# A two-layer diffusion backbone on one core: where the gate blocks, the query sums, the second norm's root and the token weights stand

## The chip, the cores and the metric

The kernel runs on one core of one Trainium2 chip. TensorE (PE) multiplies, with its weight loads (PEld) shown apart; VectorE (DVE), ScalarE (ACT) and GpSimd (POOL) do the rest; SyncE (SP) issues the DMA loads from one in-order queue. The metric is the device time of one execution in microseconds (us), and the median over several executions is compared.

## The reference

Two layers run over 512 latent tokens and 256 context tokens of width 1024. Each layer is a half-step feed-forward, a mixing part, and a second half-step feed-forward; ahead of each stands an RMS norm with a shift and a scale, behind each a gate, all nine of them made from a conditioning vector.

```python
def half_ffn(h, g, shift, scale, gate, wg, wu, wd):
    return h + 0.5 * gate * swiglu(modulate(rms_norm(h, g), shift, scale), wg, wu, wd)

for l in range(DEPTH):
    need_ctx = l < DEPTH - 1
    ml = jnp.split(s_lat @ w_mod[l] + b_mod[l], N_MOD, axis=-1)     # mc: the same from s_ctx
    x = half_ffn(x, ..., ml[0], ml[1], ml[2], ...)                  # ctx with mc
    y_l, y_c = token_mixing(modulate(rms_norm(x, ..), ml[3], ml[4]), ...)
    x = x + ml[5] * y_l
    x = half_ffn(x, ..., ml[6], ml[7], ml[8], ...)                  # ctx too if need_ctx
```

`token_mixing` projects the tokens, runs six heads of grouped-query attention, a short gated convolution and six heads of latent attention (its queries come from a normed, compressed 384-wide query), and projects the concatenation back. In the last layer the context is not carried on past the keys and values.

## The kernel before, in words

Activations lie transposed: eight tiles `xT[k]` of 128 features by 768 tokens (latent and context). Every fp32 weight and activation is split into a high and a low part (`wh`/`wl`, or two slots `s`); a product is three matmuls, high by high, high by low, low by high (`mm3`). A weight block is loaded to `wr` (two buffers), cast by ACT to the high part, and subtracted by DVE to give the low part (`wsplit`). PSUM has two large buffers (`ps`) and four small ones (`po`). Buffers of a tag are used in turn. An instruction issued while an engine is "chained" keeps the written order on that engine; elsewhere a scheduler orders the instructions by readiness and written order.

The 128 modulation blocks (`mod_queue`) are taken in a fixed order, each with one load to `mr` (two buffers) and one or two sums on DVE (`junk`, one for each of the two conditioning vectors). `pump(n)` takes the next `n` blocks, `pump(upto=...)` all up to a named one. `(l, 8)` is the gate of the second feed-forward of layer `l`. `mixing` pumps up to `(l, 5)`, `(l, 7)` and `(l, 6)` at its end, and then calls `residual` for the output projection with `npump=1`: one block behind each of the five output tiles that come before the held ones. `ffn` pumps up to its gate after its first chunk of activations, ahead of the first update of `xT`.

`residual` multiplies activations by a down or output projection, adds the gated result to `xT`, and makes the normed input `h` of the next part. It has two streams of columns, `c0` (latent) and `c1` (context; in the last mixing part, the two halves of the latent tokens). The last `ntail` output tiles are held: 6 in a feed-forward that is followed by another part, 3 in the output projection. Their `c0` columns are done first; their `c1` columns are cut into units, one for each held tile and input block, which `run(n)` strews as filler on PE. The tail then goes:

- `run(4)`, and the column sums of the squares of `c0` on PE (`count_steps`, matmuls with a vector of ones); the mean and the root on DVE (`rsqrt`, eight small instructions); `run(7)`; the spread of the root by four transposes; `run(5)`.
- a loop over `k` from 0 to 8: `scaled(k)` (DVE), `high(k)` (ACT), `low(k-1)` (DVE) make `h`; `products(k-1)` on PE are the first products of the next part with blocks `E`; updates and squares of `c1` and `run(3)` come behind them. From `k == 2` on the squares of `c1` are counted, and at `k == 7` the mean and root of `c1` are made and spread. `hold` is 4 with six held tiles, 6 with three: products past it come after the spread. With three held tiles the third block of `E` is cast and subtracted at `k == 6`.
- a loop over `k` for `h` in `c1`, in which the first feed-forward's tail also prepares the token weights (`wn_late`, one 384-wide block for each `k`, `LATE`).

`mixing` makes the token projections from those blocks, the compressed keys and queries (`comp`, loop over `i`), and their sums of squares (`stats`). Just ahead of attention stand `evac`, the splits of keys and queries, `uq(0)` (the first tile of up-projected queries, with the counts of the query's squares between its products) and the mean. `attend` then runs the units, each with two query blocks: `scores`, `maxima` (DVE), `exps` (ACT), `transposes`, `high`, `low`, `values`. Further work is put at places of a unit by `at(n, place, ...)` ("mid", "b", "end"); `uq(1)` stands at unit 0's "mid".

Of the kernel before, what the change touches and what calls it, by code (L numbers as in the profile page):

```python
# [8 lines left out]
F32 = mybir.dt.float32  # L9
F32R = mybir.dt.float32r  # L10
I32 = mybir.dt.int32
AF = mybir.ActivationFunctionType
# [3 lines left out]
P = 128  # L16
D = 1024
KD = D // P
SEQ = 512
CTX = 256  # L20
T = SEQ + CTX
NLT = SEQ // P
NT = T // P
# [15 lines left out]
NWR = 2  # L39
DUE = (1, 1, 1, 1, 2)  # L40
PRE = {1: (0, 1), 5: (2,), 7: (3,)}
LAG = 1
LATE = {k: 1 for k in range(8)}
NATIVE = (0, 2)


# [1 line left out]
def tile_net(ctx: ExitStack, tc: tile.TileContext, a, out):  # L48
    nc = tc.nc
# [33 lines left out]
    te, ve, se, pe = Engine(nc.tensor, "te"), Engine(nc.vector, "ve"), Engine(nc.scalar, "se"), nc.gpsimd  # L83

    const = ctx.enter_context(tc.tile_pool(name="const", bufs=1))
    pool = ctx.enter_context(tc.tile_pool(name="pool", bufs=1))
# [4 lines left out]
    def nm(s):  # L91
        uid[0] += 1
        return f"{s}{uid[0]}"

    def slot(dt=F32, w=T):
        return pool.tile([P, w], dt, name=nm("s"), tag="s", bufs=NSLOT)
# [4 lines left out]
    def small(w, dt=F32, tag="sm", bufs=12):  # L101
        return pool.tile([P, w], dt, name=nm("m"), tag=tag, bufs=bufs)
# [7 lines left out]
    def f32(t):  # L110
        return t.bitcast(F32)
# [11 lines left out]
    zeros = const.tile([P, 2 * NT], F32, name="zeros")  # L123
# [69 lines left out]
    def wload(src, w):  # L193
        raw = pool.tile([P, 1024], F32, name=nm("wr"), tag="wr", bufs=NWR)
        nc.sync.dma_start(out=raw[:, :w], in_=src)
        return raw

    def wsplit(raw, w, hi=None, lo=None, eng=None):
        if hi is None:
            hi = pool.tile([P, 1024], F32R, name=nm("wh"), tag="wh", bufs=3)  # L200
            lo = pool.tile([P, 1024], F32R, name=nm("wl"), tag="wl", bufs=3)
        se.copy(hi[:, :w], raw[:, :w])
        (eng or ve).tensor_sub(lo[:, :w], raw[:, :w], f32(hi)[:, :w])
        return hi, lo
# [21 lines left out]
    def wblock(src, w=1024):  # L226
        return wsplit(wload(src, w), w)
# [89 lines left out]
    def rsqrt(ms, n, tag="rs", bufs=3):  # L317
        y, steps = rsqrt_steps(ms, n, tag, bufs)
        for f in steps:
            f()  # L320
        return y

    class Stats:
# [41 lines left out]
        def sums(self, *more):  # L365
            self.zero()
            for n, sq in enumerate((self.acc,) + more):
                self.count(sq, n == len(more))
# [53 lines left out]
    def residual(blocks, rhs, gate, streams, nxt, pre=None, late={}, view=nv, npump=0, ntail=3):  # L422
# [7 lines left out]
        ntail = ntail if two else 0  # L430
# [13 lines left out]
        S = [Stats(cols, D, (po, ps)[n]) for n, (cols, i) in enumerate(streams)]  # L444
# [11 lines left out]
        raws = [wload(src, 1024) for src in pre[:2]]  # L456
        E = []
# [22 lines left out]
        s1, ready, tiles = [], [], {}  # L480
        units = [(n, k) for n in range(ntail) for k in range(nk)]

        def run(count):
            for _ in range(count):
                if not units:
                    return
                n, k = units.pop(0)
                if k == 0:
                    if n % 2 == 0:
                        tiles[n // 2] = ps()  # L490
                project(packed(tiles[n // 2][:, BANK * (n % 2):BANK * (n % 2 + 1)], c1, view), held[n][1], rhs, [k])
                if k == nk - 1:
                    ready.append(n)
# [20 lines left out]
                s1.append(sq)  # L514

        squared = [0, None]
        run(4)
        for n, f in enumerate(S[0].count_steps(S[0].acc, S[0].sq)):
            f()
            if n % 3 == 2:  # L520
# [18 lines left out]
        hold = 4 if ntail == 6 else 6  # L539
        prev = None  # L540

        def products(k):
            for n in range(len(accs)):
                lat_mm(accs[n], E[n], h, k, c0, hview)

        for k in range(KD + 1):
            if k < KD:
                cur = HMod(h[k], k, c0, R, A[i0][:, k:k + 1], B[i0][:, k:k + 1], hview)
                cur.scaled()
                cur.high()  # L550
            if k == 6 and len(E) == 2:
                E.append(wsplit(raws[2], 1024))
            if prev is not None:
                prev.low()
                if k <= hold or k == KD:
                    products(k - 1)
            prev = cur
            second_update()
            second_square()
            run(3)  # L560
            if k == 2:
                S[1].zero()
                S[1].count(S[1].acc, False)
            if k >= 2:
                for _ in range(2 if k < 7 else len(s1)):
                    if s1:
                        S[1].count(s1.pop(0), not (s1 or ready or updated or units))
            if k == 7:

                S[1].mean()  # L570
                r1 = rsqrt(S[1].ms, S[1].w // P)
                R1 = po()
                for j in range(S[1].w // P):
                    te.transpose(out=R1[:, j * P:(j + 1) * P], in_=r1[:, j:j + 1].to_broadcast([P, P]), identity=ident)
                if len(accs) == 2:
                    accs.append(po())
                    for kk in range(hold):
                        lat_mm(accs[2], E[2], h, kk, c0, hview)
                for kk in range(hold, 7):
                    products(kk)  # L580
        prev = None
        for k in range(KD + 1):
            if k < KD:
                cur = HMod(h[k], k, c1, R1, A[i1][:, k:k + 1], B[i1][:, k:k + 1], hview)
# [6 lines left out]
            prev = cur  # L591
# [598 lines left out]

    def wn_late(l, wn):

        k, both = len(wn), slot(F32R)
        hi, lo = both[:, 0:384], both[:, 384:768]
        wn.append((hi, lo))
        raw = wload(a["wiN"][l, k, :, 0:384], 384)
        se.copy(hi, raw[:, 0:384])
        return lambda: ve.tensor_sub(lo, raw[:, 0:384], f32(hi))

    def mixing(l, hin, early, streams, nxt, pre):  # L1200
        h, E, accs = hin
# [53 lines left out]
        for c0, w, nt in ((0, 384, nqt), (384, 288, NT)):  # L1255
            if c0:
                conv(1)
            wn = []
            for k in range(KD):
                wn.append(early.pop(0) if c0 == 0 and early else wn_block(l, k, c0, w))  # L1260
            for t in range(nt):
# [21 lines left out]
                lo = 0 if t < nqt else 384  # L1283
# [87 lines left out]
        for i in range(5):  # L1371
            name, g, w = ("ckv", gckv[:, i:i + 1], T) if i < 2 else ("cq", gcq[:, i - 2:i - 1], wq)
            pt = ps()
            project(natural(pt, slice(0, w)), wb, h,
                    between=stats["ckv"].count_steps(stats["ckv"].acc, stats["ckv"].sq) if i == 3 else ())
            if i < 4:
                wb = wblock(a["wiT"][l, i + 1])
            else:
                wuq.append(wsplit(wload(a["wuq"][l, 0], 864), 864,
                                  *(pool.tile([P, 1024], F32R, name=nm("we"), tag="mr", bufs=2) for _ in range(2))))  # L1380
                wuq.append(wblock(a["wuq"][l, 1], 864))
            for f, t in ramp[i]:
                f(t)
            if i == 3:
                stats["ckv"].mean()
            elif i == 4:
                rr["ckv"] = rsqrt(stats["ckv"].ms, NT)
            if i < 4:
                evac(pt, name, g, w)
                stats[name].square(pt[:, :w])  # L1390
                if i != 1:
                    stats[name].accumulate()
# [42 lines left out]
        key_split(k1, slot(F32R), pool.tile([P, T], F32R, name=nm("k2"), tag="mscr", bufs=1))  # L1435
        query_split(q0, 1)
        stats["cq"].accumulate()


        st3 = pool.tile([P, NT, 18], F32, name=nm("st3"), tag="st3", bufs=1)  # L1440
# [19 lines left out]
        def uq(t, between=()):  # L1460
            q = slot()
            q_tok.append(q)
            sq = temp()
            pt = ps().rearrange("p (f c) -> p f c", f=2)
            up([pt[:, f, :288] for f in range(2)], t, comp["cq"], 288, wuq, between)
            se.copy(q[:, :576].rearrange("p (f c) -> p f c", f=2), pt[:, :, :288])
            se.activation(out=sq[:, :576].rearrange("p (f c) -> p f c", f=2), in_=pt[:, :, :288], func=AF.Square)
            sv = sq[:, :576].rearrange("p (h d) -> p h d", d=96)

            def sums():  # L1470
                ve.tensor_reduce(out=st3[:, t, 0:6], in_=sv[:, :, 0:64], axis=AX.X, op=ALU.add)
                ve.tensor_reduce(out=st3[:, t, 6:12], in_=sv[:, :, 64:96], axis=AX.X, op=ALU.add)
            return sums
# [86 lines left out]
        def load_ukv(hf):  # L1560
            wukv.append(wblock(a["wukv"][l, hf], 768))

        sums = uq(0, stats["cq"].count_steps(stats["cq"].acc))
        stats["cq"].mean()
        sums()
        unchain("te", "ve", "se")


# [63 lines left out]
        def at(n, place, f, *args):  # L1632
            jobs.setdefault((n, place), []).append(lambda: f(*args))

        def up_at(n, f, t):
            def start():
                jobs.setdefault((n, "end"), []).insert(0, f(t))
            at(n, "mid", start)

        per = 3 if need_ctx else 2  # L1640
        up_at(0, uq, 1)
        at(0, "end", lambda: uq(2)())
        up_at(1, uq, 3)
        if need_ctx:
            at(1, "end", lambda: uq(4)())
# [63 lines left out]
        pump(upto=(l, 5))  # L1709
        pump(upto=(l, 7))  # L1710
        pump(upto=(l, 6))
        return residual(lambda o: first_out[0] if o == 0 else wblock(a["wo"][l, o]), rhs, (l, 5), streams, nxt, pre, npump=1)

    def cst(name, l, shape):
        t = pool.tile(shape, F32, name=nm(name), tag=name, bufs=1)
# [273 lines left out]
```

## Time and profile before

| | us |
|---|---|
| median of 3 runs | 2800.01 (2799.33 to 2801.71) |
| the profiled execution | 2797.64 |
| its span, first to last instruction | 2795.8 |
| PE busy in it | 2696.0 |
| DVE busy | 1944.1 |
| ACT busy | 1089.0 |
| POOL busy | 146.9 |

A timeline row has the start, the length, the engine, the operation with its output and input tiles, the number of merged instructions, and in brackets how long the engine had been idle and what ended that. In a table of stretches each engine has its busy time; behind POOL stand the granted clock of PE (1.00 is full), the busy share of the DMA engines and their GB/s. Matmuls of a row overlap, so a row is somewhat longer than its share of time. An fp32 matmul that is not split shows as two instructions. Nearly all instructions go through one helper and have its line, L66, so the tile names tell them apart: `ps`, `po` PSUM tiles, `m` small vectors, `t` temporaries, `s` slots, `junk` the output of the modulation sums.

By stage: the first feed-forward of layer 0 runs to about 600, mixing to about 944, the output projection to 1035, the second feed-forward to about 1575, the first of layer 1 to 2100, its mixing to 2371, its output projection to 2430, and the last feed-forward to the end.

### The profile page before, as it was taken

What the parts mean: (1) busy time and instruction counts of PE and PEld (TensorE: products, weight loads), DVE (VectorE), ACT (ScalarE), POOL (GpSimd) and SP (SyncE); (2) the same over time, 40 slices, a digit from 0 to 9 for tenths busy, and PEclk for the clock granted to TensorE, in tenths of its full rate; (3) what the DMA queues carried; (4) which work ended last, traced back from release to release, by engine and by line L of the source; (5) the groups of instructions that cost most, each with busy time, mean ns of one, the idle gap of its engine ahead of it and who ended that gap; (6) DMA issues with size and microseconds to landing.
All of it is one profiled execution on the core that took longest, in us unless ns stands there. A gap on an engine that the chain in (4) does not pass through costs nothing. (4 is left out here: it accounts for less than half of the span.)

```text
span 2795.8 us, 38908 instructions
## 1 busy us (share of the span) xinstructions
PE 2696.0 (96%) x15440; PEld 2515.6 (90%) x15440; DVE 1944.1 (70%) x3293; ACT 1089.0 (39%) x1860; POOL 146.9 (5%) x194
## 2 busy tenths in 40 slices
PE   8999999999889998999999999999999999999999
PEld 5999999988788888999999899999988788888887
DVE  6857777777688866777777777777766798633333
ACT  5223333341478532333334333333342477322221
POOL 0000000001132200000000000000000233000000
PEclk9999999999999999999999999999999999999999
DMA  7313333233000321333333133333225101232332
GB/s 245 121 56 103 106 106 106 83 103 115 29 2 9 106 77 53 98 106 107 107 107 102 50 94 107 109 107 108 86 64 172 32 9 56 90 104 91 91 98 91
DMA packets 95269, 251.80 MB, mean 90 GB/s; under 512 B 11376, under 2 KB 40816, under 8 KB 95088
## 3 DMA queue, kind: packets, MB, share of 16 engines
q1 hardware_dynamic: 95088, 249.33, 28.2%
q8 instruction: 121, 1.98, 0.3%
q14 instruction: 60, 0.49, 0.1%
HBM read 247.19 MB, written 2.10 MB: 89 GB/s over the span
## 5 line engine op out<-in xcount | busy, mean ns | idle before, releaser
L66 PE MATMUL ps<-s,wh 128*128 128x384 f32 (+2 forms) x4724 | 1146.5, 349 | 17.3 <-DVE xT L66 11.9
L66 PEld LDWEIGHTS ps<-s,wh 128*128 128x128 f32 x4724 | 832.7, 188 | 90.2 <-issue 15.1
L66 PE MATMUL ps<-s,wl 128*128 128x384 f32 (+2 forms) x2362 | 707.4, 347 | 0.3 <-DVE wl L66 0.3
L66 PE MATMUL po<-s,wh 128*128 128x384 f32 (+2 forms) x2476 | 643.7, 341 | 2.4 <-ACT t L66 1.7
L66 PEld LDWEIGHTS po<-s,wh 128*128 128x128 f32 x2476 | 447.0, 188 | 15.6 <-ACT t L66 2.7
L66 PEld LDWEIGHTS ps<-s,wl 128*128 128x128 f32 x2362 | 428.7, 188 | 32.7 <-DVE wl L66 0.8
L66 PE MATMUL po<-s,wl 128*128 128x384 f32 (+2 forms) x1238 | 422.2, 341 | 0.3 <-DVE wl L66 0.3
L66 ACT CAST wh<-wr 128x1024 fp32r<-128x1024 f32 (+5 forms) x219 | 209.1, 957 | 449.1 <-PE ps L66 319.1
L66 DVE TENSOR_TENSOR wl<-wr,wh 128x1024 fp32r<-128x1024 f32 (+5 forms) x219 | 243.3, 1113 | 194.1 <-ACT wh L66 191.8
L66 DVE SCALAR_TENSOR_TENSOR xT<-ps,mod,xT 128x256 f32<-128x256 f32 (+1 forms) x392 | 212.6, 585 | 193.8 <-PE ps L66 191.9
L66 DVE SCALAR_TENSOR_TENSOR junk<-mr,sb 128x1024 fp8e4<-128x1024 f32 x224 | 273.4, 1221 | 16.4 <-DMA mr<-in_wm_dram 15.5
L66 PEld LDWEIGHTS po<-s,wl 128*128 128x128 f32 x1238 | 232.2, 188 | 6.7 <-DVE wl L66 0.5
L66 PE MATMUL po<-s,s 128*128 128x256 f32 (+3 forms) x952 | 157.6, 316 | 9.6 <-DVE t L66 3.7
L66 PEld LDWEIGHTS po<-s,s 128*128 128x128 f32 x952 | 140.5, 190 | 17.7 <-ACT s L66 6.5
L66 ACT COPY t<-po 128x384 f32<-128x384 f32 (+1 forms) x161 | 76.9, 478 | 195.2 <-PE po L66 194.2
L66 ACT ACTIVATE t<-t 128x384 f32<-128x384 f32 x106 | 55.7, 526 | 238.2 <-DVE t L66 238.2
L66 DVE TENSOR_TENSOR t<-ps,t 128x384 f32<-128x384 f32 (+3 forms) x91 | 55.3, 608 | 112.3 <-PE ps L66 110.3
L66 DVE TENSOR_TENSOR s<-t,s 128x768 fp32r<-128x768 f32 (+2 forms) x129 | 98.6, 767 | 41.0 <-ACT s L66 40.8
L66 ACT CAST s<-t 128x768 fp32r<-128x768 f32 (+2 forms) x129 | 87.9, 684 | 97.2 <-DVE t L66 96.9
L66 PE MATMUL po<-s,w 128*128 128x384 f32 x636 | 119.7, 336 | 0.0
L66 PE MATMUL po<-ident,t 128*128 128x128 f32 x684 | 101.7, 280 | 13.9 <-ACT t L66 12.9
L66 DVE TENSOR_TENSOR t<-po,t 128x384 f32<-128x384 f32 (+2 forms) x169 | 94.0, 557 | 28.6 <-ACT t L66 28.0
(180 smaller groups left out, 3094.6 us busy)
## 6 DMA issues: line engine op xcount, KB each, us to landing
mr<-in_wm_dram SPq DMA_DIRECT2D x128, 512.0 KB, 3.7
wr<-in_wg_dram SPq DMA_DIRECT2D x88, 512.0 KB, 3.5
wu<-in_wu_dram SPq DMA_DIRECT2D x53, 512.0 KB, 3.6
t<-in_wd_dram SPq DMA_DIRECT2D x56, 384.0 KB, 3.4
wr<-in_wu_dram SPq DMA_DIRECT2D x35, 512.0 KB, 3.5
wr<-in_wiT_dram SPq DMA_DIRECT2D x22, 512.0 KB, 3.5
wr<-in_wd_dram SPq DMA_DIRECT2D x16, 512.0 KB, 3.5
wr<-in_wo_dram SPq DMA_DIRECT2D x14, 512.0 KB, 4.0
```

Of the source, the lines that this page charges most:

```text
L66: f(*args, **kw)
```

## The change

`LATE` names four places instead of eight, and `wn_late` loads two blocks at once and casts and subtracts both together. In `residual` eight units run ahead of the first counts where six tiles are held; the third block is cast at `k == 4` and subtracted at `k == 5`; the counts of `c1` begin at `k == 1`, its mean and root are made at `k == 6`; and `products(k-1)` come behind the updates, the units and the counts of the same `k`. In `mixing` the root of `ckv` moves from the loop's end to behind the last accumulation, where a one-column Exp is added; the counts of the query's squares move from `uq(0)` to `uq(1)`, their mean to unit 1; and `npump` is 2.

```diff
-LATE = {k: 1 for k in range(8)}
+LATE = {0: 1, 2: 1, 4: 1, 6: 1}
...
         squared = [0, None]
-        run(4)
+        run(8 if ntail == 6 else 4)
         for n, f in enumerate(S[0].count_steps(S[0].acc, S[0].sq)):
...
+        third = []
         for k in range(KD + 1):
             if k < KD:
                 cur = HMod(h[k], k, c0, R, A[i0][:, k:k + 1], B[i0][:, k:k + 1], hview)
                 cur.scaled()
                 cur.high()
-            if k == 6 and len(E) == 2:
-                E.append(wsplit(raws[2], 1024))
+            if k == 4 and len(E) == 2:
+                third.extend(pool.tile([P, 1024], F32R, name=nm(t), tag=t, bufs=3) for t in ("wh", "wl"))
+                se.copy(third[0], raws[2])
             if prev is not None:
                 prev.low()
-                if k <= hold or k == KD:
-                    products(k - 1)
-            prev = cur
+            if k == 5 and third:
+                ve.tensor_sub(third[1], raws[2], f32(third[0]))
+                E.append(tuple(third))
             second_update()
             second_square()
             run(3)
-            if k == 2:
+            if k == 1:
                 S[1].zero()
                 S[1].count(S[1].acc, False)
-            if k >= 2:
-                for _ in range(2 if k < 7 else len(s1)):
+            if k >= 1:
+                for _ in range(2 if k < 6 else len(s1)):
                     if s1:
                         S[1].count(s1.pop(0), not (s1 or ready or updated or units))
-            if k == 7:
-
+            if k == 6:
                 S[1].mean()
                 r1 = rsqrt(S[1].ms, S[1].w // P)
+            if prev is not None and (k <= hold or k == KD):
+                products(k - 1)
+            prev = cur
+            if k == 7:
+
                 R1 = po()
...
-        k, both = len(wn), slot(F32R)
-        hi, lo = both[:, 0:384], both[:, 384:768]
-        wn.append((hi, lo))
-        raw = wload(a["wiN"][l, k, :, 0:384], 384)
-        se.copy(hi, raw[:, 0:384])
-        return lambda: ve.tensor_sub(lo, raw[:, 0:384], f32(hi))
+        k, hi, lo = len(wn), slot(F32R), slot(F32R)
+        wn.extend((hi[:, c:c + 384], lo[:, c:c + 384]) for c in (0, 384))
+        raw = pool.tile([P, 1024], F32, name=nm("wr"), tag="wr", bufs=NWR)
+        nc.sync.dma_start(out=raw[:, :T].rearrange("p (o c) -> p o c", o=2),
+                          in_=a["wiN"][l, k:k + 2, :, 0:384].rearrange("o p c -> p o c"))
+        se.copy(hi, raw[:, :T])
+        return lambda: ve.tensor_sub(lo, raw[:, :T], f32(hi))
...
             if i == 3:
                 stats["ckv"].mean()
-            elif i == 4:
-                rr["ckv"] = rsqrt(stats["ckv"].ms, NT)
...
         query_split(q0, 1)
         stats["cq"].accumulate()
+        se.activation(out=small(1), in_=zeros[:, 0:1], func=AF.Exp)
+        rr["ckv"] = rsqrt(stats["ckv"].ms, NT)
...
-        sums = uq(0, stats["cq"].count_steps(stats["cq"].acc))
-        stats["cq"].mean()
-        sums()
+        uq(0)()
...
-        up_at(0, uq, 1)
+        up_at(0, lambda t: uq(t, stats["cq"].count_steps(stats["cq"].acc)), 1)
         at(0, "end", lambda: uq(2)())
+        at(1, "b", lambda: stats["cq"].mean())
...
-        return residual(..., (l, 5), streams, nxt, pre, npump=1)
+        return residual(..., (l, 5), streams, nxt, pre, npump=2)
```

2 lines of the change are left out of this document (1 added, 1 removed).

## The prediction

> **What bounds the kernel now.** I read the page's head, then TensorE's (PE's) waits over the span, then the granted clock, then the timeline around each long wait.
>
> ```profile
> span 2795.8 us, 38908 instructions
> ...
> PE 2696.0 (96%) x15440; PEld 2515.6 (90%) x15440; DVE 1944.1 (70%) x3293; ACT 1089.0 (39%) x1860; POOL 146.9 (5%) x194
> ```
>
> PE is busy for 96%. The change takes no product away, so it can win only in PE's 100 us of idle time (2795.8 - 2696.0) and where PE runs at a lower clock. From the waits of PE (us in total, times, longest):
>
> ```profile
> PE ps L66 <- DVE xT L66: 11.9, 4, 10.3
> ...
> PE po L66 <- DVE m L66: 9.2, 6, 1.9
> ```
>
> The first is one wait of 10.3; the second is six waits, five of them for the second norm's root (1.5 to 1.9 each). Next, stretches of the span; the column PEclk (last but two) is the granted clock:
>
> ```profile
> 734.60:741.00 6.40, 6.40 (x29) 6.40 (x30) 0.17 (x1) 0.00 (x0) 0.00 (x0) 0.50 0.00 0
> 1086.50:1090.50 4.00, 3.98 (x13) 4.00 (x14) 4.00 (x8) 0.83 (x1) 0.00 (x0) 0.54 0.00 0
> 1544.00:1547.00 3.00, 2.92 (x14) 2.92 (x15) 2.72 (x13) 1.45 (x3) 0.00 (x0) 0.52 0.00 0
> 2104.50:2107.50 3.00, 3.00 (x10) 3.00 (x11) 1.41 (x5) 1.39 (x3) 0.00 (x0) 0.53 0.89 354
> ```
>
> PE is "busy" here but at half clock: each stretch follows a stall. A long stall costs its length and then half of the next 3 to 8 us.
>
> **Query sums in attention, layer 0.** Timeline (start, duration, engine, operation, [idle before]):
>
> ```profile
> 727.59 1.47 PE L66 MATMUL po<-ident,s 128*128 128x128 f32 x12
> ...
> 729.35 0.81 ACT L66 ACTIVATE t<-ps 128x768 f32<-128x768 f32 x1
> ...
> 731.77 0.60 PE L66 MATMUL po<-zeros,ident 128*128 128x12 f32 x2 [2.71 <-DVE k L66]
> ...
> 733.13 0.96 DVE L66 TENSOR_TENSOR s<-s,t 128x768 f32<-128x768 f32 x1
> ...
> 734.14 0.59 PE L66 MATMUL po<-ones,s 128*128 128x2 f32 x2 [1.76 <-DVE s L66]
> ...
> 741.19 1.24 PE L66 MATMUL ps<-k,s 128*128 128x512 f32 x4
> ...
> 742.67 1.45 PE L66 MATMUL ps<-we,s 128*128 128x288 f32 x9 [0.24 <-ACT t L66]
> ...
> 743.38 0.95 DVE L66 TENSOR_REDUCE m<-ps 128x1 f32<-128x768 f32 x1
> ...
> 744.41 1.28 ACT L66 ACT_TABLE_LOAD   x1 [1.07 <-DVE m L66]
> ...
> 746.75 0.97 PE L66 MATMUL ps<-k,s 128*128 128x512 f32 x4 [1.43 <-ACT t L66]
> ```
>
> PE's transposes end at 729.06. Then it waits for a `po` buffer (2.71) and for the sum of squares (1.76) although the products of `uq(0)`, queued behind, need neither. Without the counts they need only the `ps` buffer that the square frees at 730.16. Eighteen products at the later pitch (1.45/9 = 0.16, overlap taken off 0.145) take 2.6: 732.8; scores of unit 0: 733.7. ACT, idle from 731.8, runs the added dummy Exp with its 1.28 load to 733.3, then copy and square to 734.5. DVE ends the accumulation at 734.1, then the moved root of `ckv` (eight small ones at 0.2, 1.6) at 735.7, sums 736.5, maxima 737.5; exp ends at 738.6. Meanwhile PE, in order, meets the moved counts in `uq(1)`: they wait for the accumulation (734.1), behind them stand `uq(1)` and the second scores. Seven steps of about 0.23 and 2.6 of products end near 738.7. The second scores start there, not at 746.75: **-8.0**. The dummy is free as ACT is idle; without that cover it costs 1.28. The mean, moved to unit 1, is one small DVE instruction; the maxima behind it would wait for the counts, which ended a unit earlier.
>
> Layer 1 likewise:
>
> ```profile
> 2200.66 0.74 DVE L66 SCALAR_TENSOR_TENSOR s<-ps,gcq,s 128x512 fp32r<-128x512 f32 x1
> ...
> 2201.49 0.60 ACT L66 ACTIVATE t<-ps 128x512 f32<-128x512 f32 x1 [0.61 <-DVE s L66]
> ...
> 2205.52 0.59 PE L66 MATMUL po<-ones,s 128*128 128x2 f32 x2 [4.79 <-DVE s L66]
> ...
> 2216.22 0.96 PE L66 MATMUL ps<-k,s 128*128 128x512 f32 x4 [0.37 <-ACT t L66]
> ```
>
> The root of `ckv`, eight small instructions, stood just ahead of the row at 2200.66; moved, it lets this row, the square and the accumulation (ended before 2205.52) go 1.0 sooner. By the same steps `uq(0)` starts near 2201.1, the accumulation ends at 2204.4, root, sums and maxima at 2207.7 (1.6, 0.8, 0.95), exp at 2208.8, and the second scores start near 2209.0: **-7.2**. Bounds per layer: the idle alone, -4.5, to -9.5.
>
> **Gate blocks.**
>
> ```profile
> 1072.97 1.22 DVE L66 SCALAR_TENSOR_TENSOR junk<-mr,sb 128x1024 fp8e4<-128x1024 f32 x1
> ...
> 1085.23 2.19 DVE L66 SCALAR_TENSOR_TENSOR xT<-ps,mod,xT 128x512 f32<-128x512 f32 x4
> ...
> 1086.52 1.62 PE L66 MATMUL ps<-s,wh 128*128 128x384 f32 x4 [10.25 <-DVE xT L66]
> ...
> 1615.36 0.94 PE L66 MATMUL ps<-s,wh 128*128 128x384 f32 x4 [0.47 <-DVE xT L66]
> ...
> 944.00:985.00 41.00, 41.00 (x235) 35.63 (x234) 32.42 (x53) 9.93 (x15) 0.00 (x0) 1.00 0.44 144
> ```
>
> In layer 0 the eight gate blocks (0,8) need eight pumps, and the output projection gives five. The other three are six sums of 1.22 from 1072.97 on, ahead of the first update (1085.23), and PE stands 10.25. With `npump=2` all eight (and two of the next layer's) are done before. The same place in layer 1 has its gate early and waits 0.47: -9.8, and 4.00 us at clock 0.54 give back 1.8: **-11.6**. What moves: ten more sums, 11.8 at their pitch, into the stretch 944 to 985 where DVE has 41.0 - 32.4 = 8.6 free. So 3.2 may stick out ahead of the low halves of the held weights; the bounds are 0 and 11.8, and as 15 us of the held blocks follow, I take **+1.0**. Each pump also issues one load on SP, so five more stand there ahead of later `wo` loads; a load that waits for one of the two `mr` buffers holds those behind it, and through them PE's weights, which is the same 0 to 11.8. No edit touches POOL's queue. In layer 1 the list of blocks is two further on, so its output projection has less to do, and its last feed-forward none before as after: 0.
>
> **Tails: root sooner, units, third block.**
>
> ```profile
> 570.83 0.61 PE L66 MATMUL po<-ones,s 128*128 128x2 f32 x4 [1.18 <-DVE s L66]
> ...
> 1021.55 1.23 DVE L66 TENSOR_TENSOR wl<-wr,wh 128x1024 fp32r<-128x1024 f32 x1 [1.73 <-ACT wh L66]
> ...
> 1023.50 0.73 PE L66 MATMUL po<-s,we 128*128 128x512 f32 x2 [0.98 <-DVE s L66]
> ...
> 1026.46 0.43 PE L66 MATMUL po<-ident,m 128*128 128x128 f32 x2 [1.53 <-DVE m L66]
> ...
> 1544.08 0.76 PE L66 MATMUL ps<-s,wh 128*128 128x256 f32 x2 [0.58 <-DVE xT L66]
> ...
> 2090.12 0.16 DVE L66 TENSOR_SCALAR m<-ps 128x2 f32<-128x2 f32 x1 [2.02 <-PE ps L66]
> ...
> 2092.00 0.40 PE L66 MATMUL po<-ident,m 128*128 128x128 f32 x2 [1.92 <-DVE m L66]
> ...
> 2421.08 0.86 PE L66 MATMUL po<-s,we 128*128 128x256 f32 x5 [1.50 <-DVE s L66]
> ...
> 2423.61 0.40 PE L66 MATMUL po<-ident,m 128*128 128x128 f32 x2 [1.67 <-DVE m L66]
> ```
>
> The mean at 2090.12 waits 2.02 for counts that stand on PE behind `products(3)`; the transposes at 2092.00 wait for the chain of nine small instructions from it, 1.9 us. After the change the counts of a tile go ahead of its products and begin at tile 1, so the sum is complete by tile 3, and the chain runs on DVE right after `low(5)`, while PE still has `products(2)` and `products(3)`, eighteen products of 512 columns (an estimate of some 4 us by the 0.145 for 288 columns). The 1.92 goes in each of the three feed-forward tails (-5.8). What is late next: the chain puts `scaled(7)` and `low(6)` back by 1.8, but they are wanted only after 27 more products, some 6 us: 0.
>
> Four more units ahead of the first count fill its 1.18 wait (-1.2). In the other two tails, with four activation blocks, eight units complete the first two held blocks, so that the half written tile is no longer read in between: the 0.58 wait goes twice (-1.2), and with it the 3.00 at clock 0.52 that followed the first one (-1.5). There the first count starts later; DVE's first `scaled` may come 0.6 later, but PE has the earlier counts as cover: 0, at worst +0.6 each. The counts themselves only change place; where PE meets one before its square is made, it waits for one update and one square, some 0.9.
>
> In the tails of the output projection the third block's cast is issued two tiles sooner and its subtraction a tile later than the cast, so DVE no longer waits 1.73 for it ahead of `low(5)`: -2.5 in layer 0 (0.98 and 1.53). In layer 1 the tiles are half as wide, PE runs out of products before DVE gets to the chain, and the last square is counted ahead of `products(2)`: of 1.50 and 1.67 I take about half, -1.5 (0 to -3.2). Sum **-13.7**.
>
> **Token weights in pairs.**
>
> ```profile
> 2103.81 0.48 DVE L66 SCALAR_TENSOR_TENSOR t<-xT,mod,po 128x256 f32<-128x256 f32 x1
> ...
> 2104.43 3.84 PE L66 MATMUL po<-s,s 128*128 128x384 f32 x13 [3.66 <-DVE t L66]
> ```
>
> PE waits for the `po` buffer of the spread root, freed by the last `scaled` (2103.81), which trails eight casts, subtractions and loads through two buffers. With four pairs, two are loaded ahead, and the other two go out when DVE has subtracted the first two. DVE then has 15 instructions 0.4 apart (0.48 long, overlapping) and four of 0.95 (as 768 columns take at 733.13), 9.8. The spread at 2092.00 comes 2.5 sooner (1.92 and 0.58), the loop starts near 2090.0 and frees the buffer at 2099.8. PE, which stood from 2100.77 (2104.43 - 3.66), arrives at 2098.3 and waits 1.5: -2.2, and 3.00 at clock 0.53 give -1.4: **-3.6** (0 to -5.1). In layer 0 nothing waits there: 0.
>
> **Sum.** -8.0 - 7.2 - 11.6 + 1.0 - 13.7 - 3.6 = -43.1. The profiled execution took 2797.6 (span 2795.8 and 1.8 around it): 2754.5. The median shown, 2800.0, is 2.4 above it: **2757**.
>
> **A rule against the trace.** The stall that I leave at attention's start is short by the rows:
>
> ```profile
> 2200.60:2202.00 1.40, 0.13 (x3) 0.04 (x1) 1.40 (x3) 0.79 (x3) 0.00 (x0) 1.00 0.81 226
> ...
> 2203.00:2205.00 2.00, 0.00 (x0) 0.00 (x0) 1.95 (x4) 0.58 (x1) 0.00 (x0) 0.50 0.00 0
> ```
>
> The clock fell more than 1.4 and less than 2.4 us after the transposes ended at 2200.6; the change leaves PE idle 1.1 in layer 0 and 0.5 in layer 1, so I keep full clock. The Trainium skill ("TensorE: Matmul & The Clock Gate", Part 1) has the clock halve after one idle window of about 3.4 us that runs freely, and says that transposes do not count as busy. The rows cannot refute that, as transposes ran right up to the idle stretch.
>
> As a rival in rows: if the clock falls once PE has had no products for some 3 us, layer 0's gap, at least 2.6 (727.59 to 730.2), may be enough, and `uq(0)` starts at 0.50 as 734.60 to 741.00 did. Its 2.6 become 5.2, of which DVE's chain hides about half: +1.5, 2758.
>
> **Rivals.** (1) *DVE fills the output projection*: all 11.8 lands on PE, or update 0 still waits behind the `sums`: +11, **2768**. For it: only 8.6 free. Against: held blocks need the low halves one by one. (2) *Attention sets its own pace*: ACT or DVE gives back the head start, the idle alone is won in no layer: +15, **2772**. Against: DVE and ACT stood idle too. (3) *Slower*: buffers of `po` turn in another order (the sums' tile is now taken inside the loop) and each of the 60 units waits longer for its transposes. It decides from 43.1/60 = 0.72 us a unit; at 0.9 it gives +54 - 43.1: **2811**. Against: the buffer comes free in unit 1, one of four. (4) *The change doesn't do what it says*: the root chain still ends after product 3, and the tails win nothing: +13.7, **2771**.
>
> **How the numbers follow.** Forecast 0.50, of this the halved clock 0.10; (1) 0.14, (2) 0.12, (4) 0.07; two of these together (2780 to 2786) 0.07; within 0.2% 0.03; (3) 0.04; 0.03 remains for more than I sum, down to 2744 by the outer bounds. 0.2% is 5.6 us, about what a measurement here can tell. Range 2744 to 2784; the likeliest's own is 2748 to 2766. Faster 0.93, same 0.03, slower 0.04.
>
> **What would show it.** Right: no `po<-zeros` wait before `uq(0)`; PE at 1.00 there; no wait over 1 us at the first residual of layer 0's second feed-forward; no wait for `m` in five tails; the token products' wait under 2. Wrong: a wait for `wl` or `xT` at the held blocks, or attention's stretch as long as before plus the head start.

## The result, and the profile after

The changed kernel takes 2753.4 us (median of 4 runs, 2750.0 to 2756.4) against 2799.7 us before: a ratio of 0.9833, 95% interval 0.9816 to 0.985. Measured a second time, beside the experiments, the ratio was 0.982 (0.9803 to 0.9836). The forecast was 2757 with a range of 2744 to 2784.

The profiled execution took 2753.3 us. The head of its page:

```profile
span 2751.5 us, 38860 instructions
...
PE 2682.0 (97%) x15440; PEld 2503.2 (91%) x15440; DVE 1944.4 (71%) x3285; ACT 1087.5 (40%) x1854; POOL 145.7 (5%) x194
```

The span is 44.3 shorter. PE's idle time (span less busy time) went from 99.8 to 69.5, so 30.3 of it are waits. The other 14.0 are busy time: the same 15440 products ran in 2682.0 instead of 2696.0 us. Some 8 of them are clock: behind the first 50 us PE was busy at half clock for 37.8 us before and for 21.9 after, and half of that is lost. Most of the rest was won at full clock, in stretches that the change does not touch, where the products came a little faster (the last section has more on this).

The timeline of the changed kernel at the places that the prediction named (start, duration, engine, operation, idle time before it and what ended it):

```profile
578.09 0.39 PE L66 MATMUL ps<-zeros,ident 128*128 128x4 f32 x2 [1.24 <-DVE xT L66]
...
591.50 0.38 PE L66 MATMUL po<-ident,m 128*128 128x128 f32 x2
...
724.71 1.47 PE L66 MATMUL po<-ident,s 128*128 128x128 f32 x12
...
727.12 1.46 PE L66 MATMUL ps<-we,s 128*128 128x288 f32 x9 [0.94 <-DVE k L66]
...
733.47 0.96 DVE L66 TENSOR_REDUCE m<-ps 128x1 f32<-128x768 f32 x1
...
736.89 0.64 ACT L66 COPY s<-ps 128x576 f32<-128x576 f32 x1 [4.54 <-PE ps L66]
...
737.43 0.91 ACT L66 ACTIVATE t<-ps,m 128x768 f32<-128x768 f32 x1
...
738.48 0.97 PE L66 MATMUL ps<-k,s 128*128 128x512 f32 x4 [1.62 <-ACT t L66]
...
1015.27 0.38 PE L66 MATMUL po<-ident,m 128*128 128x128 f32 x2
...
1065.45 0.94 PE L66 MATMUL ps<-s,wh 128*128 128x384 f32 x4 [0.49 <-DVE xT L66]
...
1536.31 0.38 PE L66 MATMUL po<-ident,m 128*128 128x128 f32 x2
...
2059.03 0.38 PE L66 MATMUL po<-ident,m 128*128 128x128 f32 x2
...
2069.30 0.93 PE L66 MATMUL po<-s,s 128*128 128x384 f32 x4 [1.51 <-DVE t L66]
...
2171.65 0.96 PE L66 MATMUL ps<-k,s 128*128 128x512 f32 x4
...
2379.65 0.41 PE L66 MATMUL po<-ident,m 128*128 128x128 f32 x2 [0.90 <-DVE m L66]
```

The reader is to see four things. The transposes of the second root (591.50, 1015.27, 1536.31, 2059.03) no longer wait for `m`; only the last tail keeps 0.90. The wait of 10.25 at the first residual of layer 0's second feed-forward is 0.49. The token products wait 1.51; the prediction had worked out 1.5. And two things are new: a wait of 1.24 at 578.09, where the counts now begin, and, at attention's start in layer 0, a first exp (737.43) that stands behind a copy (736.89), although the maxima that it needs ended at 734.43 (733.47 + 0.96).

The ten sums that moved into the output projection cost PE nothing, as the same stretch of that stage shows (columns: window, PE, PEld, DVE, ACT, POOL busy, granted clock, DMA share, GB/s):

```profile
936.00:977.00 41.00, 41.00 (x234) 35.62 (x233) 39.44 (x68) 10.28 (x15) 0.00 (x0) 1.00 0.59 184
```

DVE is busy 39.44 of 41.0 us, was 32.42, and PE does not wait once. That is six of the ten sums; the last four run behind the stretch, from 977 to 985, where PE does not wait either.

### The profile page after: what moved, and what is told of

Read it like the earlier page. It is cut to its first block, busy times and chain, and to the rows that moved or that the text cites. A ratio compares the mean times of both kernels' runs of the same rounds, so it can differ in the third digit from the quotient of the medians.

```text
span 2751.5 us, 38860 instructions
## 1 busy us (share of the span) xinstructions
PE 2682.0 (97%) x15440; PEld 2503.2 (91%) x15440; DVE 1944.4 (71%) x3285; ACT 1087.5 (40%) x1854; POOL 145.7 (5%) x194
## 5 line engine op out<-in xcount | busy, mean ns | idle before, releaser
L66 DVE TENSOR_REDUCE m<-ps 128x1 f32<-128x768 f32 (+1 forms) x120 | 101.0, 841 | 20.4 <-PE ps L66 19.9
```

Of the source, the lines that this page charges most:

```text
L66: f(*args, **kw)
```

## The experiments

All times are medians. Each ratio is to the kernel before in runs beside it on the same chip, with its 95% interval; 0.001 is 2.8 us.

| run | median | before | ratio |
|---|---|---|---|
| gate_only | 2788.8 | 2803.0 | 0.9952 (0.9936 to 0.9968) |
| sums_only | 2787.0 | 2803.0 | 0.9949 (0.9935 to 0.9964) |
| tails_only | 2782.6 | 2803.0 | 0.9934 (0.992 to 0.9949) |
| pairs_only | 2805.6 | 2803.0 | 1.001 (0.9996 to 1.0024) |
| after_again | 2750.7 | 2801.0 | 0.982 (0.9803 to 0.9836) |
| exp_first | 2754.7 | 2801.0 | 0.9836 (0.9818 to 0.9853) |
| late_last | 2752.9 | 2801.0 | 0.9826 (0.981 to 0.9842) |
| fill_wait | 2797.9 | 2801.0 | 0.9988 (0.9975 to 1.0001) |
| filled | 2747.7 | 2798.3 | 0.9811 (0.9793 to 0.9829) |
| after_no_pairs | 2760.9 | 2798.3 | 0.9862 (0.9841 to 0.9883) |
| counts_alone | 2783.2 | 2798.3 | 0.9943 (0.9924 to 0.9961) |
| count_later | 2756.0 | 2798.3 | 0.9844 (0.9823 to 0.9865) |

**The four parts, each alone on the kernel before.** First the gate blocks:

```diff
-        return residual(..., (l, 5), streams, nxt, pre, npump=1)
+        return residual(..., (l, 5), streams, nxt, pre, npump=2)
```

> The kernel before with two pumps a block in the output projection and nothing else. Theory A (the parts stand side by side, each worth what its own stage showed): the wait of 10.25 at the first residual of layer 0's second feed-forward falls under 0.6 and the 4 us at clock 0.54 behind it go; the ten more sums hide. 11 to 12 us faster than before, near 2788. Rival B (DVE fills the output projection, the sums only change their place): a new wait of several us at its held blocks, 0 to 4 us faster, 2796 to 2800.

It was 13 us faster (9 to 18). Its timeline at the residual:

```profile
1079.75 0.93 PE L66 MATMUL ps<-s,wh 128*128 128x384 f32 x4 [0.44 <-DVE xT L66]
```

The wait of 10.25 is 0.44, and no other took its place: theory A.

The query sums alone were the attention hunks of the change (counts given to `uq(1)`, mean in unit 1, dummy Exp and root of `ckv` behind the accumulation).

> The kernel before with the attention part alone: counts of the query sums in the second query block, mean in unit 1, the root of ckv and a dummy Exp behind the accumulation. Theory A: 12 to 13 us faster, near 2787, of it about 5.4 in layer 0 and 7.3 in layer 1; in layer 0 the copy of the second query block again stands ahead of the first exp on ACT. Rival B (the gain at attention's start came from the earlier arrival out of shorter tails, or from the table load alone): at most 4 us faster, 2796 or more.

14 us faster (10 to 18): theory A, and layer 0 falls short in the same way as in the changed kernel. In its timeline the second scores again wait for an exp that stands behind the copy:

```profile
729.78 1.47 PE L66 MATMUL po<-ident,s 128*128 128x128 f32 x12
...
732.20 1.45 PE L66 MATMUL ps<-we,s 128*128 128x288 f32 x9 [0.95 <-DVE k L66]
...
738.54 0.96 DVE L66 TENSOR_REDUCE m<-ps 128x1 f32<-128x768 f32 x1
...
741.47 0.64 ACT L66 COPY s<-ps 128x576 f32<-128x576 f32 x1 [4.04 <-PE ps L66]
...
742.00 0.91 ACT L66 ACTIVATE t<-ps,m 128x768 f32<-128x768 f32 x1
...
743.05 1.65 PE L66 MATMUL ps<-k,s 128*128 128x512 f32 x4 [1.62 <-ACT t L66]
```

The tails alone were the new body of `residual`, with the token weights still loaded tile by tile.

> The kernel before with the changed tails of the residual alone (root two tiles sooner, counts ahead of the products, eight units first, third block sooner). Theory A: the five waits for m go, 14 to 16 us faster, 2784 to 2786; the prediction's own terms for it are 13.7. Rival B (what the tails win is waited for again at the next buffer, at the token products of layer 1 and at the first residual of layer 0's second feed-forward, whose 3.66 and 10.25 stand in this kernel and hang on DVE): only 6 to 9 us faster, 2791 to 2794, and those two waits 2 us longer than before.

18 us faster (14 to 22), so more than its 13.7. Of the five waits for `m` one of 0.9 is left. But rival B is right at one of its two places. This is the timeline of the tails-only kernel where layer 1's token products begin:

```profile
2082.49 0.51 ACT L66 CAST s<-wr 128x384 fp32r<-128x384 f32 x1 [1.32 <-DMA wr<-in_wiN_dram]
...
2086.64 0.51 ACT L66 CAST s<-wr 128x384 fp32r<-128x384 f32 x1 [3.22 <-DMA wr<-in_wiN_dram]
...
2089.48 0.51 ACT L66 CAST s<-wr 128x384 fp32r<-128x384 f32 x1 [1.92 <-DMA wr<-in_wiN_dram]
...
2091.12 2.26 PE L66 MATMUL po<-s,s 128*128 128x384 f32 x6 [7.15 <-ACT s L66]
```

The wait there grew from 3.66 to 7.15. ACT stands for the weights' loads (1.32, 3.22, 1.92), which go through two buffers one tile at a time, and the high halves of the second norm queue behind those casts. So 3.5 was waited for again, as much as layer 1's tail won. About half of it came back: PE now reaches the second pass over the tokens later and waits nowhere in it, where it waited 1.85 before. A place that rival B did not name lost too: in layer 0's second pass the waits grew from 0.76 to 2.39. The other place that it named kept its 10.3.

The pairs alone:

```diff
-LATE = {k: 1 for k in range(8)}
+LATE = {0: 1, 2: 1, 4: 1, 6: 1}
...
+        nc.sync.dma_start(out=raw[:, :T].rearrange("p (o c) -> p o c", o=2),
+                          in_=a["wiN"][l, k:k + 2, :, 0:384].rearrange("o p c -> p o c"))
```

> The kernel before with the token weights in four pairs and nothing else. Theory A (eight casts, subtractions and loads set the end of the loop): the wait of 3.66 at layer 1's token products falls to 1.4 to 1.9 and the 3 us at half clock behind it go: 3 to 4.5 us faster, near 2796. Rival B (the late root sets it, since the loop can't start before): the wait stays over 3, within 1 us of before.

No gain: 1.001, so between 1 us faster and 7 slower. The timeline:

```profile
2105.84 2.32 PE L66 MATMUL po<-s,s 128*128 128x384 f32 x12 [1.51 <-DVE t L66]
...
2141.16 0.40 PE L66 MATMUL po<-s,s 128*128 128x288 f32 x1 [1.63 <-ACT s L66]
```

The wait did fall by the 2.15 of theory A. But PE then came sooner to the second pass over the tokens, which waits for its own weights (1.63, then 0.43, 0.22 and 0.71; before 0.44, 0.36 and 1.05), and 6.8 us at half clock lay there in this trace. So theory A was right on the wait and wrong on the time.

**The pairs, taken out of the changed kernel** (`LATE` and `wn_late` as before, all else changed):

> The changed kernel with the token weights loaded one tile at a time again. Theory A (the pairs are what lets the sooner root count: alone, the sooner tail only lengthened the wait at layer 1's token products from 3.66 to 7.15): the wait there is 6.5 to 7.5 instead of 1.51, 5 to 6 us slower than the changed kernel, with a window or two of half clock behind it up to 9. Rival B (the two parts are independent): the wait is 3 to 4, 2 to 3 us slower.

```profile
2073.21 1.30 PE L66 MATMUL po<-s,s 128*128 128x384 f32 x3 [6.84 <-DVE t L66]
```

6.84 against 1.51, and half clock for 6.8 us from 2070.9 on: theory A. The ratio of 0.9862 is 12 us above the second measurement of the changed kernel and 8 above the first. Over the whole trace PE waits 5.5 us longer: layer 1's second pass over the tokens gives 1.27 back, and layer 0's waits 2.29 instead of 0.64. The pairs win nothing alone, and without them about half of the sooner root's gain is left at this place; beside the sooner root the pairs are worth these 5.5 us of wait. How much more, the runs can't tell: the other three parts add to 46 us alone and give 39 together here, each figure to some 4 us.

**The changed kernel again**, unaltered, to see what differs between two executions:

> The changed kernel again, beside the next three and beside the kernel before on the same chip. Theory A (the clock is halved in whole stretches of 3.4 us, each costing 1.7 us, and which of the short waits is followed by one is chance): its runs lie several us apart, span times granted clock is the same in all of them within 3 us (near 2735), and the trace shows half clock behind other waits than the first trace of it (which had it at 580, 733, 771, 836, 911 and 2225). Rival B (each wait has its own fixed price in clock): half clock at the same six places, runs within 2 us.

Theory A: its four runs span 7.6 us. The granted clock of a run goes from 0.995 to 0.998, and span times clock lies at 2737 to 2741, in the first four at 2734 to 2741 (a clock given to 0.001 leaves 1.4 open). That is 4 us, where theory A had 3; the pace of the products differs too (last section). In its trace the half clock stood at 581, 772 and 837, not at 733, 911 or 2225.

**exp first.** On the changed kernel, an order that ACT must keep:

```diff
+            if n == 0:
+                chain("se")
             u.exps(0)
+            if n == 0:
+                unchain("se")
```

> The changed kernel with ACT's first exp of attention put ahead of the copy of the second query block. Theory A (the missing part of layer 0's term is this order on ACT): the second scores of layer 0 no longer wait 1.62 but under 0.3 and start 1.3 to 1.9 us sooner after the first query block than in the changed kernel; layer 1, where exp already went first, is unchanged; 1.5 us faster than the changed kernel. Rival B (the half clock there is what is missing, or the copy behind exp holds up the second query block's buffer): the start comes under 0.5 us sooner, or a new wait of the same size for the copied buffer follows within 5 us.

Its timeline:

```profile
724.51 1.47 PE L66 MATMUL po<-ident,s 128*128 128x128 f32 x12
...
734.32 0.90 ACT L66 ACTIVATE t<-ps,m 128x768 f32<-128x768 f32 x1 [2.88 <-DVE m L66]
...
736.66 0.87 PE L66 MATMUL ps<-k,s 128*128 128x512 f32 x4
738.11 1.45 PE L66 MATMUL ps<-we,s 128*128 128x288 f32 x9 [0.58 <-ACT t L66]
```

The wait of 1.62 is gone and the second scores start 12.15 after the transposes (724.51 to 736.66) instead of 13.77, both with one half-clocked stretch in between. 0.58 comes back at the next query block. That leaves 1 us, which the ratio cannot show (0.9836 against 0.982 and 0.9833): mechanism as theory A, size below it.

**The counts alone.** On the kernel before, only the counts and the mean were moved; no dummy Exp, the root of `ckv` in its old place:

> The kernel before with the counts of the query sums in the second query block and the mean in unit 1, but without the dummy Exp and with the root of ckv left in its old place. Theory A (each piece has its share): the waits of 2.71, 1.76 and 4.79 are gone, but ACT loads its table between the maxima and the first exp (1.28 more on the chain) and in layer 1 the accumulation ends 1 us later: 8 to 10 us faster, 3 to 4 us less than the whole attention part. Rival B (the counts are all of it): as fast as the whole attention part, 12 to 14 us.

```profile
732.92 1.47 PE L66 MATMUL po<-ident,s 128*128 128x128 f32 x12
...
740.18 0.96 DVE L66 TENSOR_REDUCE m<-ps 128x1 f32<-128x768 f32 x1
...
741.21 1.28 ACT L66 ACT_TABLE_LOAD   x1 [1.28 <-DVE m L66]
742.51 0.91 ACT L66 ACTIVATE t<-ps,m 128x768 f32<-128x768 f32 x1
...
743.55 0.97 PE L66 MATMUL ps<-k,s 128*128 128x512 f32 x4
```

Theory A fell, rival B holds: 0.9943, as fast as the whole part (0.9949). In layer 0 the second scores start 10.63 after the transposes, sooner than with the whole part (13.27, of which half clock is at most 1.9). The table load does stand ahead of exp, but the maxima come 1.5 sooner, since no root of eight instructions stands ahead of them on DVE: they start 4.84 after `uq(0)`'s products do (735.34), and 6.34 after in the run with the whole part (732.20 and 738.54). And exp runs ahead of the copy. In layer 1 the counts alone won 7.0, the whole part 7.3.

**Counting one tile later** (`k == 2` in place of `k == 1` in the tails with six held blocks):

> The changed kernel with the counts of the second norm begun one tile later (tile 2) in the tails that have six held blocks. Theory A (the new wait of 1.24 at layer 0's first tail is the price of counting at tile 1): the wait goes or shrinks under 0.5 there, and the clock stays full behind it, 1 to 3 us faster than the changed kernel. Rival B (PE would stand there for the first tile's low half anyhow, as the kernel before did with 0.32 and 0.46): a wait of about 1 us for ACT or DVE takes its place, no difference.

```profile
577.17 0.50 PE L66 MATMUL po<-s,we 128*128 128x512 f32 x1 [1.59 <-ACT s L66]
578.13 2.08 PE L66 MATMUL po<-s,we 128*128 128x512 f32 x4 [0.46 <-DVE s L66]
```

Rival B: PE would stand there for the first tile's high and low half in any case. The new wait of 1.24 costs nothing that this run can show.

**The last pair after the loop** (`LATE = {0: 1, 2: 1, 4: 1, 8: 1}`):

> The changed kernel with the last of the four weight pairs cast after the last scaled tile of the tail. Theory A (the spread root's buffer is held by the last scaled, which trails the four subtractions of 0.95): the wait of 1.51 at layer 1's token products falls by 0.9 to about 0.6, 1 us faster. Rival B (the last pair then comes late for the products of tiles 6 and 7): a new wait for it of 0.5 us or more inside the token products, no gain.

```profile
2068.78 1.45 PE L66 MATMUL po<-s,s 128*128 128x384 f32 x7 [0.43 <-DVE t L66]
...
2103.14 0.40 PE L66 MATMUL po<-s,s 128*128 128x288 f32 x1 [0.68 <-ACT s L66]
...
2106.59 3.79 PE L66 MATMUL po<-s,s 128*128 128x288 f32 x15 [0.79 <-ACT s L66]
```

The wait fell from 1.51 to 0.43, as theory A had it, and no product waited for the late pair. Yet nothing was won: waits of 0.68, 0.44, 0.37 and 0.79 stand in the second pass over the tokens, 2.28 in sum, where the changed kernel has 1.08. That pass, whose casts stand for loads, is what sets the time there now. Whether sooner loads would help was not tried.

**What an idle PE costs in clock.** On the kernel before, products that nobody reads were put ahead of the residual tile that waits 10.25:

```diff
+            if stall and o == 2:
+                filled.append(po())
+                for _ in range(54):
+                    te.matmul(out=filled[0][:, 0:HALF], lhsT=wb[0][:, 0:P], rhs=rhs[0][0][:, 0:HALF], start=True, stop=True)
```

> The kernel before with 54 products of 384 columns added on PE ahead of the residual tile that waits 10.25 us in layer 0's second feed-forward (9.4 us at 0.174 each, into a tile that nobody reads). Theory A (idle PE is what halves the clock): the wait shrinks to about 0.8, the clock stays at 1.00 behind it, and the products behind it take 1.8 to 2 us less than in the kernel before: 1 to 3 us faster for 54 products more. Rival B (the clock falls for another reason, load on DVE or a running budget): 0.5 again behind the wait, no gain or slower.

Its timeline:

```profile
1076.72 9.59 PE L66 MATMUL po<-s,wh 128*128 128x384 f32 x54
1087.17 0.94 PE L66 MATMUL ps<-s,wh 128*128 128x384 f32 x4 [0.86 <-DVE xT L66]
```

And the four microseconds behind the wait, in a row of stretches:

```profile
1087.20:1091.20 4.00, 4.00 (x23) 4.00 (x24) 3.95 (x8) 1.25 (x2) 0.00 (x0) 1.00 0.00 0
```

Theory A: a wait of 0.86, and clock 1.00 where it was 0.54. From the wait's end to the next wait of 0.57 it took 21.77 us (1087.17 to 1108.94), before 23.43 (1086.52 to 1109.95): 1.7 sooner with 54 products more. The ratio, 0.9988 (0.9975 to 1.0001), leans the same way.

**Filling by rule.** The last section works out from the traces what the clock looks at. This run used that rule on the changed kernel with exp first:

```diff
+        def fill(self, n):
+            for _ in range(n):
+                te.matmul(out=self.O[:, 256:512], lhsT=self.V(self.pv[0][0]), rhs=self.pv[0][1], start=True, stop=True)
...
             prev.values()
+            prev.fill(jobs.get((n, "fill"), 0))
```

> The changed kernel with exp put first as above and 58 products of 256 columns that nobody reads, put where PE waits anyway: 6 ahead of the counts in layer 0's unit 0 (a wait of 0.69), 10 ahead of the scores of unit 5 (1.26), 25 ahead of the transposes of unit 16 (3.11), 17 ahead of the scores of unit 8 in layer 1 (2.13). Theory A (the clock is halved for the 3.41 us after a window of a fixed grid in which PE streamed less than about 0.4 of the columns it can; products count by their columns, transposes twice theirs, counts of two columns as nothing): each place comes over 0.4, no half clock at 733, 770, 835 to 843 and 2222, where the traces so far had four to five windows, 1.7 us each: 5 to 8 us faster than the changed kernel with exp first, ratio to the kernel before near 0.980. Rival B (idle time of any length drops the clock at a chance of its own, or the added products delay what waits for them): half clock as often as before, or new waits, same or slower than the changed kernel.

```profile
828.41 3.71 PE L66 MATMUL po<-s,s 128*128 128x256 f32 x29
831.96 0.38 PE L66 MATMUL po<-ident,s 128*96 128x128 f32 x2
```

Where 3.11 us were waited, 25 products now run (29 with the four real ones), and the transposes behind them follow at once. All four places stayed at full clock in its trace. In the six traces of the changed kernel and its other variants they had half clock in two, five, six and five. Other places fell there (903, 992, 2105, 2241; 579 as before). The ratio is 0.9811, four of the five runs had a granted clock of 0.998 or 0.999, but the interval overlaps the changed kernel's. So the clock held where the rule said it would, in the one trace there is, and a gain over the changed kernel is not shown.

## Why the prediction was right, and where it was off

The sum was 43.1 and the spans differ by 44.3. The four parts alone give 13, 14, 18 and -3, together about 43 us, each to some 4 us. Term by term, from shifts between the same instructions in the two traces:

- **Gate blocks**, -11.6: measured -11.5 (1052.75 to 1109.95 before, 1041.51 to 1087.21 after). The ten sums, +1.0: 0. Four sums did stick out of the stretch (the sum had 3.2 us), but no wait on PE followed. That refutes rival 1.
- **Query sums, layer 1**, -7.2: measured -7.3.
- **Query sums, layer 0**, -8.0: -5.4 in the first trace (19.16 from transposes to second scores before, 13.77 after), -6.8 in the second (12.37). The step that failed is "sums 736.5, maxima 737.5; exp ends at 738.6": the maxima came when it said (they end 7.3 after `uq(0)` starts, in the sum and in the trace), but it took for granted that ACT runs exp next. Nothing chains ACT there, and the copy of the second query block was put first (1.62). At full clock, in the second trace, the rest of the chain was some 0.4 shorter than in the sum, so 1.2 are missing. In the first trace a stretch at half clock cost 1.4 more, and it was not the case given a chance of 0.10: that one had `uq(0)` at half clock, which ran at full clock in both traces; the fall came later, over the counts and `uq(1)`. "The dummy is free as ACT is idle" holds of its time, but with the moved root it bought nothing: the counts alone reached -8.5.
- **Tails**, -13.7: -18.7 by the shifts, in the order of the tails (L0: -3.9, -2.9, -6.7; L1: -3.5, -1.7, with what the pairs did in layer 0's first). Some 4 of this is not the change: 1.1, 2.3 and 0.6 lie ahead of the three feed-forward tails, where the two kernels do the same, so about -15 is left. The 2.3 lie in 420 us of layer 0's second feed-forward in which neither trace has a wait but the 0.57 at the start. The products there came a little faster, as two rows of the same stretch show, before and then after:

```profile
1196.00:1239.00 43.00, 43.00 (x248) 43.00 (x247) 32.47 (x56) 15.84 (x25) 0.00 (x0) 1.00 0.39 122
```

```profile
1173.26:1216.26 43.00, 43.00 (x250) 43.00 (x250) 32.87 (x55) 15.84 (x25) 0.00 (x0) 1.00 0.38 121
```

In the second trace of the changed kernel these 420 us took as long as before, to 0.2 us.

- **Pairs**, -3.6: -4.3 in the trace, with the wait of 1.51 worked out rightly. What the text did not see is that this term and layer 1's tail (-2.5) are not two. It had "the loop starts near 2090.0" and counted both; alone, the pairs won nothing and the sooner root kept about half of its gain here. "In layer 0 nothing waits there: 0" put a term at nothing: with the sooner root but no pairs, layer 0's second pass waits 1.65 longer.
- **"DVE's first `scaled` may come 0.6 later, but PE has the earlier counts as cover: 0"**: there is a new wait of 1.24, and it costs 0, but because PE had to wait for the first tile anyway, not because of the counts.
- **Clock.** The text kept full clock where PE idles less than 1.4 us. That is the wrong measure (last section): in the first trace the clock fell at 733.6 after idle stretches of 0.94 and 0.69.

These terms add to 47.2. Against them stand 1.2 us lost in the first 50 us, where the kernels are the same, and 1.6 at a half-clocked stretch at 2225, which the trace of before does not have. So that the sum met the spans to 1.2 is in part luck: 2.6 us too few in attention were made up by 4.0 of faster products that the change did not cause.

Rivals 2 and 4 are out (both attention stages won, five waits for `m` went to one), and so is the slower one (3): after attention's start, no wait of 0.9 or more in the attention units grew by more than 0.1.

## What to carry to other kernels

Where two parts of a change meet at one buffer, ask what each is worth without the other: a sooner start wins less if the loads behind it set the end. A chain of estimated times holds only as far as the order on each engine is forced; write down which engine is free to choose. And a wait costs its length and, by chance of its place on the clock's grid, 1.7 us or a multiple more, so two profiles of one kernel differ in where the clock is lost.

## What the runs showed of the hardware

Half clock comes in whole stretches of 3.41 us, on one grid for the whole of an execution. In the trace of before the stretches (from 731 us on) begin at 731.8, 779.6, 844.4, 919.5, 1079.9, 1544.1, 2103.9 and 2202.9: whole multiples of 3.4133 apart to 0.1 us. Four neighbouring windows of that grid in the kernel before, with the granted clock last but two:

```profile
1537.29:1540.70 3.41, 3.41 (x25) 3.04 (x23) 2.38 (x4) 1.26 (x2) 0.00 (x0) 1.00 0.51 154
1540.70:1544.11 3.41, 2.83 (x25) 2.63 (x24) 0.55 (x2) 0.00 (x0) 0.00 (x0) 1.00 0.02 5
1544.11:1547.52 3.41, 3.41 (x16) 3.41 (x17) 2.92 (x11) 1.65 (x4) 0.00 (x0) 0.51 0.00 0
1547.52:1550.94 3.42, 3.42 (x32) 3.42 (x32) 2.11 (x4) 1.48 (x4) 0.00 (x0) 0.99 0.53 153
```

In the second window PE was busy 2.83 of 3.41, and still the third was halved: much of it were counts, products of two columns. I took all 14 traces from 45 us on, cut each by its own grid, and counted for each window the columns of the products that began in it, as a share of 7500 (512 columns in 0.233 us at full clock). A share under 0.41, with products and counts taken by their columns and transposes at twice theirs, was followed by half clock in 132 windows and not in 11; of the 11013 windows at 0.41 or more, 7 were. Idle time alone tells less: the best limit, 1.9 us in a window, puts 69 on the wrong side, against 18. Products without transposes do badly too (330 windows under 0.41 kept full clock). The rule is fitted to these traces; the one run that was built on it held at its four places. At the start of an execution it does not hold: from 20 to 45 us, 19 of 100 windows were under 0.41, and full clock followed all of them. Why is open.

The Trainium skill ("TensorE: Matmul & The Clock Gate", Part 1) describes such free-running windows of 3413 ns, and the traces agree. The prediction put the transposes under Part 1 too; the Trainium skill speaks of them in Part 4 of that page: a transpose "doesn't count as PE-busy the same way". For the transposes of this kernel the measurement differs. In the changed kernel a window holds fifteen of them, no product, and 1.4 us of idle time, and the next window keeps full clock:

```profile
2238.96:2242.37 3.41, 2.04 (x15) 1.32 (x13) 3.35 (x11) 2.18 (x5) 0.00 (x0) 1.00 0.00 0
2242.37:2245.78 3.41, 2.90 (x23) 2.82 (x24) 2.95 (x6) 2.17 (x5) 0.00 (x0) 1.00 0.02 5
```

The size of it: the runs of before beside the second measurement had a mean span of 2799.7 and by their granted clocks lost 37.5 us of it, the changed kernel 9.6 of 2749.2. Part of the lost time falls into waits and costs nothing, so this is an upper bound, but it says that shorter waits paid twice. What PE itself lost, half of its busy time at half clock behind the first 50 us, is 18.9 in the trace of before and 11.0 and 6.5 in the two of the changed kernel. The prediction had put 4.7 us in its terms as clock by name (1.8, 1.5 and 1.4), and the rest inside its attention terms.

Products with no wait between them were not equally fast from one execution to the next. In layer 0's second feed-forward three products of 384 columns took 0.524 us before and 0.520 in the first trace of the changed kernel, but 0.524 in its second, on the mean over some 2300 products each, all at a granted clock of 1.00; the 248 and 250 products in the rows above lean the same way. What sets this is open.
